# Input stage in another order, with the input's residual scaled in DRAM's copy later, in a hybrid decoder layer

## The chip, the cores and the metric

One core of one Trainium2 chip runs the whole layer. The metric is the time of one execution in microseconds (us) of device time, as the median of several runs. The kernel before takes 1295.74 us, median of 3 runs (1294.87 to 1296.15).

## What is computed

The input is x (1 x 1024 x 1024, fp32), ahead of which 16 meta tokens are put, so 1040 rows in all. One layer runs over them; its parts, cut to what matters here:

```python
h = layer_norm(concat([meta, x]), in_ln_g, in_ln_b)
z = h @ w_in + b_in
q, k, v, c_in, gates = split(z)                       # 512, 128, 128, 1024, 2048 columns
y_attn = sliding_window_attention(q, k, v) @ w_attn_proj
c = c_val * sigmoid(c_gate)                           # the halves of c_in
y_conv = silu(layer_norm(causal_dwconv(c, 31 taps))) @ w_conv_proj
mixed = sigmoid(g_attn) * y_attn + sigmoid(g_conv) * y_conv
h = layer_norm(ALPHA * h + mixed @ w_out)             # ALPHA = 2 ** 0.25
f = (gelu(g) * u) @ ffn_w_down                        # u, g: conv3 of h @ ffn_w_up
out = layer_norm(ALPHA * h + f)                       # meta rows dropped
```

The change touches the way from x to h and to the first tiles of z, and the way from h to the term ALPHA * h, called the residual here.

## The kernel before, in words

Activations stand transposed for the products (channels on the 128 partitions, tokens along the free axis). Nearly all products run in three passes of fp32r matmuls: each operand is split into a high part, rounded to fp32r, and a low part, the rest; high times high, low times high and high times low are summed in PSUM. A split is thus a CAST and a subtraction for each operand: for activations both on DVE, for weights the cast on ACT and the subtraction on POOL (`split`, L282 and L285; in the input stage `wsplit0`, L491 and L493). A plain fp32 matmul (`raw=True`, L512) needs no split and shows two records in the trace.

A scheduler deals each engine's instructions by priority: `tc.cur_priority`, set ahead of each section and in `rank(...)` blocks; a lower number goes first, and `after(a, b)` fixes an order by hand. In the input stage the order on DVE, ACT and TensorE is written out by hand (`in_order`, `dv`, `ac`, `pe`). All loads, and stores written as `load(dram, sbuf)`, are issued in order on SP's queue (L113); `store` issues on ACT's (L117). A transfer that waits holds all behind it on its queue.

**Input stage (L171 to L560).** The rows of x come as eight blocks of 128 tokens (`load_x`), the meta tokens as a ninth, `xm`. A block's statistics (`stat`, two BN_STATS and an aggregate on DVE; `half_stat` does one half of it), an ACT table lookup and Newton steps (`table`, `newton`) give mean and rate, `norm` writes the normalised rows `xn` on DVE or ACT. `turns` transposes them on TensorE (L463), `scaled` applies the norm's gain and bias on ACT while leaving PSUM (L469, into `tm`), `parts` splits them (L479 the cast, L484 the subtraction on DVE, L482 on POOL) into RHO and RHC, the halves of h transposed, by channel blocks k = 0 to 7. Tokens go in three groups, `HG`: 272, 384 and 384 columns. Meanwhile `z_first` makes the first three column tiles of z: tile 0 is k, tile 1 is v, tile 2 is the first quarter of q (L515, or L512 raw); `evac` takes a finished tile out of PSUM. In group 0 only k runs raw, while the splits are made; v and q follow, v's weights arriving first. In group 1 v and q run together, and k behind them; in group 2 one tile after the other. POOL makes four low parts of group 2 and all three weights' low parts.

**Residual, before.** gb holds the norm's gain and bias on all partitions (1 MB, loaded in the start). Behind the input stage `residual` scales gb by ALPHA once (L269), turns each block of x in place into ALPHA * h by two operations of 128x1024 on DVE (L271, L272), and stores it in DRAM's h0d. h0d is read back as `OB<-h0d` for the product with w_out. x's buffers belong to the start's pools, whose memory goes to the convolution's input `cin` and to attention's tiles when they close.

**Convolution, gates, attention (L640 to L985).** Their tiles of z (`z_tile`, L309, L312 and L313 for the three passes, with 400, 384 and 256 columns), the taps on DVE (L677), attention on all engines.

**Projections (L1040 to L1115).** For each of eight output blocks m the joined weights w_attn_proj and w_conv_proj (`w_ab[m]`, 512 KB) are loaded and split. For each of four token groups g (`PG`, 258 or 256 columns) `branch` makes two products: attention's (PSUM tag "mm", three buffers) and the convolution's (tag "t", two buffers). `merge` loads both gates of the block from DRAM (sgd, `OB<-sgd` or `FA<-sgd`, 256 KB), then on DVE: gate times product one (L1084), gate times product two (L1085), their sum (L1086), and the split of the result, ACT's half (L1093) and DVE's subtraction (L1094). At m < 4 w_out's blocks are loaded besides.

Of the kernel before, what the change touches and what calls it, by code (L numbers as in the profile page):

```python
# [29 lines left out]
P = 128  # L30
# [34 lines left out]
RK_TURN, RK_SPLIT, RK_EVAC, RK_START, RK_QKV, RK_RESID, RK_ATT = 450, 500, 600, 1000, 10000, 20000, 30000  # L65
RK_CLN, RK_OSPLIT, RK_Z, RK_CONV, RK_PROJ = 38000, 39000, 40000, 60000, 70000
# [35 lines left out]
def tile_hybrid_layer(  # L102
# [89 lines left out]
    for j in range(NB):  # L192
        with rank((10, 11, 15, 17, 18, 20, 21, 22)[j]):
            load_x(j)
# [28 lines left out]
    nc.vector.tensor_scalar(qb, colA[:, 0:4], HD ** -0.5, None, OP.mult)  # L223

    nc.vector.tensor_scalar(colA[:, 10:30], colA[:, 10:30], 0.5, None, OP.mult)
# [3 lines left out]
    nc.vector.tensor_scalar(nsink, sink, -1.0, None, OP.mult)  # L229
# [32 lines left out]
    gb = sp.tile([P, 2, D], F, name="gb")  # L262
    load(gb[:, :, :].rearrange("p a b -> p (a b)"), dram(ln0_in, 0, [[0, P], [1, 2 * D]]))
    gb_scaled = []

    def residual(src, mu, rs, n, first, dst):
        if not gb_scaled:
            gb_scaled.append(1)
            after(nc.vector.tensor_scalar(gb, gb, ALPHA, None, OP.mult), last_split[3])  # L269
        src = src[:n]  # L270
        nc.vector.scalar_tensor_tensor(src, src, mu[:n], gb[:n, 0], OP.subtract, OP.mult)  # L271
        nc.vector.scalar_tensor_tensor(src, src, rs[:n], gb[:n, 1], OP.mult, OP.add)  # L272
        load(dst, src[first:n])

# [15 lines left out]
    def weights(shape, fill):  # L290
# [4 lines left out]
        with rank({1: 14, 2: 13, 3: 16, 4: 23}.get(n, RK_SPLIT)):  # L295
            last_fill.append(fill(raw))
# [94 lines left out]
    norms, xns, later = {}, {}, []  # L391
# [42 lines left out]

    def norm(t, j, on_dve):
# [3 lines left out]
        xns[j] = sp.tile([P, D], F, name="xn", tag="xn", bufs=4) if j >= 0 else xm  # L439
        to = xns[j] if j >= 0 else xm[96:]  # L440
# [6 lines left out]
        later.append((x_, mv[:n, i, 0:1], r_[:n, i:i + 1], n, j))  # L447
# [72 lines left out]

    def evac(g, *tiles):
        for i in tiles:
            a, b = span(i, g)
            with rank(RK_EVAC):
                evacs0[i](g, a, b, sums0[i])
# [8 lines left out]
    table(1)  # L534
    newton(1)
# [3 lines left out]
    wsplit0(1, True)  # L539
# [7 lines left out]
    parts(0, 0, 1)  # L547
    stat(2, 4)
    scaled(0, 5)
    wsplit0(2, True)  # L550
    scaled(0, 6, 7)
    z_first(0, (0,), 5, 6, 7, raw=True)
    table(2)
    parts(0, 2, 3, 4)
# [3 lines left out]
    norm(2, 4, True)  # L558
    evac(0, 0)
    parts(0, 5, 6, 7)  # L560
    z_first(0, (1,), 0, 1)
    for k in range(2, 6):
        z_first(0, (1,), k)
        z_first(0, (2,), k - 2)
    turns(1, 0, 1, 2, 3)
    scaled(1, 0, 1, 2, 3)
    wsplit0(0, True)
    z_first(0, (1,), 6)
    z_first(0, (2,), 4)
    z_first(0, (1,), 7)  # L570
    evac(0, 1)
    z_first(0, (2,), 5)
    turns(1, 4, 5, 6, 7)
    z_first(0, (2,), 6, 7)
    evac(0, 2)
    parts(1, 0, 1)
    scaled(1, 4, 5, 6, 7)
    half_stat(3, 5, 0)
    parts(1, 2)
    half_stat(3, 5, 1)  # L580
    parts(1, 3)
    half_stat(3, 6, 0)
    parts(1, 4)
    half_stat(3, 6, 1)
    parts(1, 5)
    half_stat(3, 7, 0)
    parts(1, 6)
    half_stat(3, 7, 1)
    table(3)
    parts(1, 7)  # L590
# [4 lines left out]
    for k in range(8):  # L595
        z_first(1, (1, 2), k)
    evac(1, 1, 2)
    z_first(1, (0,), 0, 1)
    turns(2, 0, 1, 2, 3)
    scaled(2, 0, 1, 2, 3)  # L600
    parts(2, 0, 1, 2, 3, on_pool=(1, 3))
    z_first(1, (0,), 2, 3, 4, 5)
    turns(2, 4, 5, 6, 7)
    scaled(2, 4, 5, 6, 7)
    parts(2, 4, 5, 6, 7, on_pool=(5, 7))
    z_first(1, (0,), 6, 7)
    evac(1, 0)
# [503 lines left out]
    for k in range(4):  # L1111
        prep_wo(k, early[k])
# [638 lines left out]
```

## Time and profile before

| what | value |
|---|---|
| median of 3 runs | 1295.74 us (1294.87 to 1296.15) |
| the profiled execution, its own time | 1294.77 us |
| its span in the trace | 1293.0 us |
| TensorE busy | 1264.6 us |
| DVE busy | 1086.4 us |
| ACT busy | 578.5 us |
| POOL busy | 66.5 us |
| moved by DMA | 212.10 MB |

The profile is one execution on the chip. PE is TensorE, DVE is VectorE, POOL is GpSimd, SP issues transfers; "SPq" is its queue of instructions. A line of a timeline has start and duration in us, engine, line of the kernel, operation, what it writes and reads, shape, count, and in brackets the idle time of the engine ahead of it with what ended it. A line of waits has engine, line and tile that waited, what it waited for, and the total, the count and the longest in us. A line of windows has the stretch, its length, each engine's busy time with the number of instructions (PE, PEld, DVE, ACT, POOL), the granted clock of TensorE, DMA's share and GB/s. Lines of DMA issues have what is written and read, queue, count, KB each, and the median us from issue to landing. The chain of waits is followed back from the last instruction to what released it.

### The profile page before, as it was taken

The numbers are of one execution on the slowest core, as the hardware profiler recorded it, in microseconds if no ns is written. First come the engines' busy times: TensorE is split into PE (matmuls) and PEld (weight loads), VectorE is DVE, ScalarE is ACT, GpSimd is POOL, SyncE is SP. The second block draws the span as 40 slices with busy tenths as digits, with TensorE's granted clock in tenths as the row PEclk, the third lists the DMA queues.
The fourth block names the chain that finished last, engine by engine and source line by source line (L and its number), as shares of the span: only waits on it lengthen the run. The fifth ranks groups of instructions, "written<-read, shape, count | busy, mean of one in ns | idle before, by whom it ended". The sixth has DMA issues, their size and how long they took to land.

```text
span 1293.0 us, 21590 instructions
## 1 busy us (share of the span) xinstructions
PE 1264.6 (98%) x8506; PEld 1186.6 (92%) x8506; DVE 1086.4 (84%) x1834; ACT 578.5 (45%) x1049; POOL 66.5 (5%) x35
## 2 busy tenths in 40 slices
PE   5999999999999999999999999999999999999997
PEld 5889999999999999788899999999999997788886
DVE  7888999999979676637899989988889876987697
ACT  4422244545554222345565554554455543535330
POOL 2200000001112232000000000000000000000000
PEclk9999999999999999999999999999999999999999
DMA  6265743433255565222135555453454566989712
GB/s 247 82 237 139 184 119 88 109 88 99 68 135 162 157 168 134 75 79 98 66 131 181 198 192 191 176 205 121 158 209 158 192 228 243 392 288 359 259 67 81
DMA packets 96008, 212.10 MB, mean 164 GB/s; under 512 B 10771, under 2 KB 35923, under 8 KB 95650
## 3 DMA queue, kind: packets, MB, share of 16 engines
q1 hardware_dynamic: 84138, 199.64, 46.3%
q10 hardware_dynamic: 11768, 11.08, 2.6%
q8 instruction: 66, 1.08, 0.4%
q14 instruction: 36, 0.29, 0.1%
HBM read 150.29 MB, written 62.70 MB: 165 GB/s over the span
## 4 chain that ended last, share of the span: by engine, by line
PE 89%; DVE 5%; DMA 4%; ACT 1%; SPq 1%; issue 0%; POOL 0%; DVEq 0%; ACTq 0%
PE px L1472 14%; PE py L1472 9%; PE ps_x L1597 9%; PE ps_z L312 7%; PE ps_z L309 7%; PE ps_z L313 7%; PE ps_z L1597 6%; PE pz L1472 5%; PE pw L1472 5%; PE ps_p L312 2%; PE ps_p L313 2%; PE ps_p L309 2%; PE ps_w L309 2%; PE ps_w L313 2%; PE ps_w L312 2%; PE ps_t L859 1%
## 5 line engine op out<-in xcount | busy, mean ns | idle before, releaser
L677 DVE SCALAR_TENSOR_TENSOR FA<-cin,cols,FA 128x1026 f32<-128x1026 f32 x120 | 154.8, 1300 | 0.2
L309 PE MATMUL ps_z<-RHO,whi 128*128 128x384 f32 (+2 forms) x324 | 104.3, 322 | 2.3 <-DVE cin L668 2.3
L312 PE MATMUL ps_z<-RHO,whi 128*128 128x384 f32 (+2 forms) x324 | 104.9, 324 | 0.0
L312 PE MATMUL ps_z<-RHC,whi 128*128 128x384 f32 (+2 forms) x324 | 104.6, 323 | 0.0
L309 PE MATMUL ps_z<-RHC,whi 128*128 128x384 f32 (+2 forms) x324 | 104.6, 323 | 0.0
L313 PE MATMUL ps_z<-RHO,wlo 128*128 128x384 f32 (+2 forms) x324 | 104.2, 322 | 0.0
L313 PE MATMUL ps_z<-RHC,wlo 128*128 128x384 f32 (+2 forms) x324 | 103.7, 320 | 0.0
L1294 DVE TENSOR_TENSOR RHO<-wr,RHO 128x512 fp32r<-128x512 f32 x94 | 63.5, 684 | 10.9 <-ACT RHO L1293 10.9
L1293 ACT CAST RHO<-wr 128x512 fp32r<-128x512 f32 x94 | 56.6, 619 | 18.6 <-DVE wr L1311 10.1
L282 ACT CAST whi<-wr 128x1024 fp32r<-128x1024 f32 x37 | 38.8, 1050 | 55.9 <-PE ps_z L312 33.5
L309 PEld LDWEIGHTS ps_z<-RHO,whi 128*128 128x128 f32 x324 | 60.9, 188 | 2.9 <-DVE cin L668 2.6
L312 PEld LDWEIGHTS ps_z<-RHC,whi 128*128 128x128 f32 x324 | 60.9, 188 | 0.6
L309 PEld LDWEIGHTS ps_z<-RHC,whi 128*128 128x128 f32 x324 | 60.8, 188 | 0.5
L313 PEld LDWEIGHTS ps_z<-RHO,wlo 128*128 128x128 f32 x324 | 60.9, 188 | 0.3
L313 PEld LDWEIGHTS ps_z<-RHC,wlo 128*128 128x128 f32 x324 | 61.0, 188 | 0.2
L312 PEld LDWEIGHTS ps_z<-RHO,whi 128*128 128x128 f32 x324 | 60.9, 188 | 0.4
L1311 DVE TENSOR_TENSOR wr<-wr 128x512 f32<-128x512 f32 x88 | 60.1, 683 | 0.2
L285 POOL TENSOR_TENSOR wlo<-wr,whi 128x1024 fp32r<-128x1024 f32 x17 | 42.1, 2479 | 186.6 <-ACT whi L282 173.6
L684 ACT ACTIVATE FA<-ps_z,cols 128x386 f32<-128x386 f32 (+2 forms) x48 | 26.1, 544 | 52.7 <-PE ps_z L313 45.0
L1484 ACT COPY FA<-px 128x514 f32<-128x514 f32 (+2 forms) x23 | 13.2, 572 | 81.3 <-PE px L1472 81.3
L1294 DVE TENSOR_TENSOR ws<-wr,ws 128x512 fp32r<-128x512 f32 x60 | 40.6, 684 | 6.1 <-ACT ws L1293 6.0
L1472 PE MATMUL px<-OA,RHO 128*128 128x258 f32 x324 | 43.5, 283 | 0.0
(452 smaller groups left out, 3593.9 us busy)
## 6 DMA issues: line engine op xcount, KB each, us to landing
wr<-in_w_up_dram SPq DMA_DIRECT2D x44, 512.0 KB, 4.1
wr<-in_w_z_dram SPq DMA_DIRECT2D x30, 512.0 KB, 3.3
fd<-FA SPq DMA_DIRECT2D x44, 256.0 KB, 2.4
OB<-in_w_down_dram SPq DMA_DIRECT2D x21, 512.0 KB, 5.0
FA<-sd SPq DMA_DIRECT2D x15, 512.0 KB, 8.8
qt<-qd SPq DMA_DIRECT2D x28, 256.0 KB, 4.1
td<-OB SPq DMA_DIRECT2D x12, 512.0 KB, 3.4
sums<-fd SPq DMA_DIRECT2D x12, 512.0 KB
```

The source lines that it names most:

```text
L282: ins = nc.scalar.copy(hi, raw)
L285: return (nc.vector if quick else nc.gpsimd).tensor_tensor(lo, raw, f32(hi), OP.subtract)
L309: ins = nc.tensor.matmul(ps, ah, bh, start=i == 0, stop=False)
L312: nc.tensor.matmul(ps, ah, bl, start=False, stop=False)
L313: last = nc.tensor.matmul(ps, al, bh, start=False, stop=i == n - 1)
L677: nc.vector.scalar_tensor_tensor(acc[c], cin[:, j:j + U], wc, acc[c], OP.mult, OP.add)
L684: nc.scalar.activation(t, ps, AF.Tanh, bias=bcol(14 + i), scale=0.5)
L1293: nc.scalar.copy(hi, src)
L1294: ins = nc.vector.tensor_tensor(lo, src, f32(hi), OP.subtract)
L1311: ins = nc.vector.tensor_tensor(*x)
L1472: ins = nc.tensor.matmul(o, x[:, ks], bmat(sub, q, hl, k), start=first and k + j == 0, stop=k == 3 and j == 2, skip_group_check=not first)
L1597: nc.tensor.matmul(banks[i], l[:, ts], r[:, ws], start=first and a and x + k == 0, stop=z and x == len(ops) - 1 and k == 2, skip_group_che ...
```

## The change

- **Loads.** Before: x0, x1, columns, v's weights, k's, x2, q's, x3 to x7. After: x0, x1, columns, k's weights, x2, x3, q's, v's, x4 to x7. The load of gb in the start is gone.
- **Order of the input stage.** q's first token group runs raw, directly behind k's; v comes last in group 0. v's low weights are made on DVE, q's and k's on POOL. Statistics are taken by whole blocks. In groups 1 and 2 the three tiles run in one interleaved loop, `lagged`, each two channel blocks behind the one before. In group 2 POOL makes no low parts any more; ACT makes four casts in its place. Three small scalings of constants move behind the first table lookup.
- **Rows to DRAM.** `norm` stores the normalised rows, without gain and bias, to h0d at once. The last four blocks of normalised rows stand in OB, not in the four buffers of `xn`.
- **Residual.** `residual(i, behind)` runs inside `merge`, at the 16 places of RES_AT: (1,0), (1,2), (2,0), (2,2), and g = 0, 1, 2 of m = 3 to 6. Each takes one half (512 channels) of a block: a load from h0d (256 KB), a multiplication by gb and an addition on DVE, and a store back to its place. At the first of each half, gb's half of gain and bias is loaded (2 x 256 KB) and scaled, and the two meta rows are done as well. There are two buffers for the rows. The loads have the merges' rank.

The added operations' places in DVE's order, as the scheduler deals them: gb's scaling and the first half block (with the meta rows) stand ahead of the first merge of all, then come one in m = 1 (at g = 3), two in m = 2, three in m = 3 (g = 1, 2, 3), two in m = 4 with gb's second scaling, two in m = 5, three in m = 6, the last two in m = 7. The multiplication stands between L1086 and L1094 of a merge or next to them, the addition beside it. On SP's queue the half blocks' stores and loads stand between the gate loads, w_ab's and w_out's.

```diff
-RK_TURN, RK_SPLIT, RK_EVAC, RK_START, RK_QKV, RK_RESID, RK_ATT = 450, 500, 600, 1000, 10000, 20000, 30000
-RK_CLN, RK_OSPLIT, RK_Z, RK_CONV, RK_PROJ = 38000, 39000, 40000, 60000, 70000
+RK_TURN, RK_SPLIT, RK_EVAC, RK_START, RK_QKV, RK_VROW, RK_ATT = 450, 500, 600, 1000, 10000, 20000, 30000
+RK_CLN, RK_OSPLIT, RK_Z, RK_CONV, RK_PROJ, RK_RESID = 38000, 39000, 40000, 60000, 70000, 200000
...
     for j in range(NB):
-        with rank((10, 11, 15, 17, 18, 20, 21, 22)[j]):
+        with rank((10, 11, 14, 15, 18, 20, 21, 22)[j]):
             load_x(j)
...
-    gb = sp.tile([P, 2, D], F, name="gb")
-    load(gb[:, :, :].rearrange("p a b -> p (a b)"), dram(ln0_in, 0, [[0, P], [1, 2 * D]]))
-    gb_scaled = []
-
-    def residual(src, mu, rs, n, first, dst):
-        if not gb_scaled:
-            gb_scaled.append(1)
-            after(nc.vector.tensor_scalar(gb, gb, ALPHA, None, OP.mult), last_split[3])
-        src = src[:n]
-        nc.vector.scalar_tensor_tensor(src, src, mu[:n], gb[:n, 0], OP.subtract, OP.mult)
-        nc.vector.scalar_tensor_tensor(src, src, rs[:n], gb[:n, 1], OP.mult, OP.add)
-        load(dst, src[first:n])
...
-        with rank({1: 14, 2: 13, 3: 16, 4: 23}.get(n, RK_SPLIT)):
+        with rank({1: 13, 2: 17, 3: 16, 4: 23}.get(n, RK_SPLIT)):
...
+    def scalings():
+        dv(V.tensor_scalar(qb, colA[:, 0:4], HD ** -0.5, None, OP.mult))
+
+        dv(V.tensor_scalar(colA[:, 10:30], colA[:, 10:30], 0.5, None, OP.mult))
+        dv(V.tensor_scalar(nsink, sink, -1.0, None, OP.mult))
+
     def norm(t, j, on_dve):
         x_, n = src_of(j)
         i = tokens[t].index(j)
         mv, t_, r_, m_ = norms[t]
-        xns[j] = sp.tile([P, D], F, name="xn", tag="xn", bufs=4) if j >= 0 else xm
-        to = xns[j] if j >= 0 else xm[96:]
+        if j < 0:
+            xns[j], to = xm, xm[96:]
+        else:
+            xns[j] = to = sp.tile([P, D], F, name="xn", tag="xn", bufs=4) if j < 4 else OB[:, (j - 4) * D:(j - 3) * D]
         for a in range(0, D, 512):
             if on_dve:
                 dv(V.tensor_scalar(to[:, a:a + 512], x_[:, a:a + 512], r_[:n, i:i + 1], m_[:n, i:i + 1], OP.mult, OP.add))
             else:
                 ac(nc.scalar.activation(to[:, a:a + 512], x_[:, a:a + 512], AF.Identity, bias=m_[:n, i:i + 1],
                                         scale=r_[:n, i:i + 1]))
-        later.append((x_, mv[:n, i, 0:1], r_[:n, i:i + 1], n, j))
+        load(*((h0d[2 + j * P:2 + (j + 1) * P, :], to) if j >= 0 else (h0d[0:2, :], xm[96 + U0:96 + NMETA])))
...
+    def lagged(g, tiles, steps):
+
+        for t in steps:
+            for l, i in enumerate(tiles):
+                if 0 <= t - 2 * l < KC:
+                    z_first(g, (i,), t - 2 * l)
+                    if t - 2 * l == KC - 1:
+                        evac(g, i)
...
+    scalings()
     newton(1)
     norm(1, 0, True)
     norm(1, 1, False)
     turns(0, 0, 1, 2, 3)
-    wsplit0(1, True)
     stat(2, 2, 3)
     scaled(0, 0)
     z_first(0, (0,), 0, raw=True)
         scaled(0, k + 1)
         turns(0, k + 4)
         z_first(0, (0,), k + 1, raw=True)
-    parts(0, 0, 1)
+    scaled(0, 5, 6)
+    parts(0, 0)
     stat(2, 4)
-    scaled(0, 5)
-    wsplit0(2, True)
-    scaled(0, 6, 7)
+    table(2)
+    scaled(0, 7)
     z_first(0, (0,), 5, 6, 7, raw=True)
-    table(2)
-    parts(0, 2, 3, 4)
+    parts(0, 1)
     newton(2)
     norm(2, 2, True)
     norm(2, 3, False)
     norm(2, 4, True)
+    z_first(0, (2,), *range(8), raw=True)
     evac(0, 0)
-    parts(0, 5, 6, 7)
-    z_first(0, (1,), 0, 1)
-    for k in range(2, 6):
-        z_first(0, (1,), k)
-        z_first(0, (2,), k - 2)
+    wsplit0(1)
+    parts(0, 2, 3, 4, 5)
     turns(1, 0, 1, 2, 3)
     scaled(1, 0, 1, 2, 3)
+    z_first(0, (1,), 0, 1, 2, 3)
+    evac(0, 2)
+    parts(0, 6, 7)
+    turns(1, 4, 5, 6, 7)
+    z_first(0, (1,), 4, 5, 6, 7)
+    evac(0, 1)
+    parts(1, 0, 1)
+    wsplit0(2, True)
+    scaled(1, 4, 5, 6, 7)
+    stat(3, 5)
+    parts(1, 2, 3)
     wsplit0(0, True)
-    z_first(0, (1,), 6)
-    z_first(0, (2,), 4)
-    z_first(0, (1,), 7)
-    evac(0, 1)
-    z_first(0, (2,), 5)
-    turns(1, 4, 5, 6, 7)
-    z_first(0, (2,), 6, 7)
-    evac(0, 2)
-    parts(1, 0, 1)
-    scaled(1, 4, 5, 6, 7)
-    half_stat(3, 5, 0)
-    parts(1, 2)
-    half_stat(3, 5, 1)
-    parts(1, 3)
-    half_stat(3, 6, 0)
-    parts(1, 4)
-    half_stat(3, 6, 1)
-    parts(1, 5)
-    half_stat(3, 7, 0)
-    parts(1, 6)
-    half_stat(3, 7, 1)
+    stat(3, 6)
+    parts(1, 4, 5)
+    stat(3, 7)
+    parts(1, 6, 7)
     table(3)
-    parts(1, 7)
     newton(3)
     norm(3, 5, True)
     norm(3, 6, False)
     norm(3, 7, True)
-    for k in range(8):
-        z_first(1, (1, 2), k)
-    evac(1, 1, 2)
-    z_first(1, (0,), 0, 1)
+    lagged(1, (1, 2, 0), range(9))
     turns(2, 0, 1, 2, 3)
     scaled(2, 0, 1, 2, 3)
-    parts(2, 0, 1, 2, 3, on_pool=(1, 3))
-    z_first(1, (0,), 2, 3, 4, 5)
+    parts(2, 0, 1, 2, 3, hi_act=(1, 3))
+    lagged(1, (1, 2, 0), range(9, 11))
     turns(2, 4, 5, 6, 7)
+    lagged(1, (1, 2, 0), range(11, 12))
     scaled(2, 4, 5, 6, 7)
-    parts(2, 4, 5, 6, 7, on_pool=(5, 7))
-    z_first(1, (0,), 6, 7)
-    evac(1, 0)
-    for i in range(3):
-        z_first(2, (i,), *range(8))
-        evac(2, i)
+    parts(2, 4, 5, 6, 7, hi_act=(5, 7))
+    lagged(2, (0, 1, 2), range(12))
     first_nm = dv_done[-1]
 
-    tc.cur_priority = RK_RESID + 1000
+    tc.cur_priority = RK_VROW
     vrow = sp.tile([NH, J_LEN], F, name="vrow")
...
-    tc.cur_priority = RK_RESID
-    for src, mu, rs, n, j in later:
-        if j >= 0:
-            residual(src, mu, rs, n, 0, h0d[2 + j * P:2 + (j + 1) * P, :])
-        else:
-            residual(src, mu, rs, NMETA, U0, h0d[0:2, :])
     start.close()
...
+    res_stack = ExitStack()
+    res_p = res_stack.enter_context(tc.tile_pool(name="res", bufs=1, side="left", reuse_waits="tile"))
+    RES_AT = [(m, g) for m in range(1, 7) for g in ((0, 2) if m < 3 else (0, 1, 2))]
+    res_gb = []
+
+    def residual(i, behind):
+        h, j = divmod(i, NB)
+        hs = slice(h * 512, (h + 1) * 512)
+        pieces = [((3, 7, 2, 6, 0, 4, 1, 5)[j], P)] + ([(-1, 2)] if j == 0 else [])
+        if j == 0:
+            res_gb[:] = [res_p.tile([P, 2, 512], F, name="gb", tag="gb")]
+            with rank(RK_EVAC):
+                for q in range(2):
+                    load(res_gb[0][:, q], dram(ln0_in, q * D + h * 512, [[0, P], [1, 512]]))
+            behind = nc.vector.tensor_scalar(res_gb[0], res_gb[0], ALPHA, None, OP.mult)
+        gb = res_gb[0]
+        for tile_, n in pieces:
+            rows = h0d[2 + tile_ * P:2 + (tile_ + 1) * P, hs] if tile_ >= 0 else h0d[0:2, hs]
+            t = res_p.tile([P, 512], F, name="res", tag="res", bufs=2)[:n]
+            with rank(RK_EVAC):
+                load(t, rows)
+            for op, q in ((OP.mult, 0), (OP.add, 1)):
+                ins = nc.vector.tensor_tensor(t, t, gb[:n, q], op)
+                after(ins, behind)
+                behind = ins
+            load(rows, t)
...
-                nc.vector.scalar_tensor_tensor(mixed2(g, m, 1), v, 0.5, f32(h), OP.mult, OP.subtract)
+                last_dve = nc.vector.scalar_tensor_tensor(mixed2(g, m, 1), v, 0.5, f32(h), OP.mult, OP.subtract)
+            if (m, g) in RES_AT:
+                residual(RES_AT.index((m, g)), last_dve)
             return ins, last_act
...
+    res_stack.close()
```

More of the change, by code (lines that the diff above doesn't have):

```diff
@@ L222, in tile_hybrid_layer @@
     qb = const.tile([P, 4], F, name="qb")
-    nc.vector.tensor_scalar(qb, colA[:, 0:4], HD ** -0.5, None, OP.mult)
-    nc.vector.tensor_scalar(colA[:, 10:30], colA[:, 10:30], 0.5, None, OP.mult)
     half_ = const.tile([P, 1], F, name="half")
@@ L228, in tile_hybrid_layer @@
     nsink = const.tile([P, NH], F, name="nsink")
-    nc.vector.tensor_scalar(nsink, sink, -1.0, None, OP.mult)
     def ln_stats(srcs, pool=None, tag="", bufs=4, behind=None, half_stats=None):
@@ L390, in tile_hybrid_layer @@
     tokens = [(-1,), (0, 1), (2, 3, 4), (5, 6, 7)]
-    norms, xns, later = {}, {}, []
+    norms, xns = {}, {}
     def src_of(j):
```

## The prediction

> **What bounds the kernel now.** First the page: busy shares, then the shares of the chain that ended last.
>
> ```profile
> PE 1264.6 (98%) x8506; PEld 1186.6 (92%) x8506; DVE 1086.4 (84%) x1834; ACT 578.5 (45%) x1049; POOL 66.5 (5%) x35
> ...
> PE 89%; DVE 5%; DMA 4%; ACT 1%; SPq 1%; issue 0%; POOL 0%; DVEq 0%; ACTq 0%
> ```
>
> TensorE is busy for all but 28 us of 1293.0, and the chain runs through it. The change takes next to nothing from TensorE's work, so it can win only where TensorE waits, and can lose wherever it makes TensorE wait. Next, therefore, TensorE's waits (times in us: total, count, longest):
>
> ```profile
> PE ps_h L463 <- DMA cols<-in_cols_dram: 8.3, 1, 8.3
> PE ps_h L463 <- DVE xn L443: 2.9, 1, 2.9
> PE ps_z L309 <- DVE cin L668: 2.3, 1, 2.3
> PE ps_z L515 <- DVE RHC L479: 1.8, 1, 1.8
> PE pw L1472 <- ACT FA L1274: 0.9, 1, 0.9
> PE ps_t L859 <- ACT pmT L782: 0.7, 1, 0.7
> ```
>
> The first two are the first loads and norms, whose order stays. The third is the bubble ahead of the first convolution tile, the fourth lies in the input stage; these two the change touches. Between 100 us and the projections nothing over 0.7 us can be won.
>
> **Part 1, the input stage: from 12 to 65 us.** A busy TensorE isn't a dense one here; what sets the pace is DVE, which splits each transposed column block (a CAST and a TENSOR_TENSOR), takes the statistics and norms. Rows of the timeline of DVE (start, duration):
>
> ```profile
> 14.45 1.29 DVE L405 BATCH_NORM_STATS2 st<-x 128x6 f32<-128x512 f32 x2 [0.95 <-DMA x<-in_x_dram]
> 15.77 0.21 DVE L406 BATCH_NORM_AGGREGATE mv<-st 128x2 f32<-128x12 f32 x1
> 15.89 0.27 DVE L479 CAST RHO<-FA 128x272 fp32r<-128x272 f32 x1
> ...
> 16.55 0.29 DVE L479 CAST RHO<-FA 128x272 fp32r<-128x272 f32 x1
> ...
> 22.71 0.15 DVE L430 SCALAR_TENSOR_TENSOR t<-mv,r 128x3 f32<-128x3 f32 x1
> ...
> 23.49 1.91 DVE L443 TENSOR_SCALAR xn<-x,r,m 128x512 f32<-128x512 f32 x4
> ...
> 30.23 0.36 DVE L479 CAST RHO<-tm 128x384 fp32r<-128x384 f32 x1 [2.77 <-ACT tm L469]
> ...
> 31.10 0.35 DVE L479 CAST RHO<-tm 128x384 fp32r<-128x384 f32 x1
> ...
> 32.94 2.77 DVE L484 TENSOR_TENSOR RHO<-tm,RHO 128x384 fp32r<-128x384 f32 x1
> ...
> 57.73 1.23 DVE L285 TENSOR_TENSOR wlo<-wr,whi 128x1024 fp32r<-128x1024 f32 x1 [2.75 <-ACT whi L282]
> ```
>
> Prices: statistics of one block 1.5 us (1.29 and 0.21); a split of 272 columns 0.66 (15.89 to 16.55), of 384 columns 0.87 (30.23 to 31.10); newton 0.8 (22.71 to 23.49); two blocks normed 1.9; a split that meets a weight split on POOL 2.77 where about 0.6 is usual (0.87 less the cast's 0.35, rounded up), 2.2 more; a weight's low half on DVE 1.2 (57.73). The stage ends on TensorE:
>
> ```profile
> 33.37 0.51 PE L515 MATMUL ps_z<-RHO,whi 128*128 128x384 f32 x2
> ...
> 33.90 0.51 PE L515 MATMUL ps_z<-RHO,whi 128*128 128x384 f32 x2
> ...
> 45.91 1.47 PE L463 MATMUL ps_h<-cols,xn 128*128 128x128 f32 x12
> ...
> 64.98 0.34 PE L309 MATMUL ps_z<-RHO,whi 128*128 128x400 f32 x1
> ```
>
> One k-step (three matmuls) takes 0.53 us (33.37 to 33.90), twelve transposes 1.47, and the first matmul after the stage starts at 64.98.
>
> Now the same walk in the new order. With x3 loaded ahead of q's weights the 0.95 wait falls away: the statistics are done at 15.0. Then split 0 (15.7), block 4 (17.2), split 1 (17.8), newton (18.6), norms (20.5), v's low half on DVE (1.2) and about 0.8 of waiting for ACT's high half (an allowance of mine) to 22.5, six splits at 0.66 and one small subtraction of 0.5 (27.0), split (1,0) (27.9), split (1,1) with a POOL lock (31.0), block 5 (32.5), two splits (34.3), block 6 (35.8), split (1,4) with k's POOL lock (38.9). TensorE has then done 6 of the 48 k-steps of groups 1 and 2, since tiles start two steps apart; the other 42 are 22.3 us, 24 transposes 2.9, end 64.1; with half a lock fewer (a lock's length depends on where the split meets it) 63.0. I take 63.0: **gain 2.0**. The later splits (0.87, against 1.6 us of matmuls for one step of three tiles) don't bind. Ends: a whole lock missed and the other halved, 4.2; both whole and a slow clock, 0 (after the next rows).
>
> ```profile
> 18.21 2.00 PE L512 MATMUL ps_z<-FA,wr 128*128 128x272 f32 x8
> ...
> 25.66 1.07 PE L515 MATMUL ps_z<-RHC,whi 128*128 128x272 f32 x2 [1.84 <-DVE RHC L479]
> ...
> 27.41 2.41 PE L463 MATMUL ps_h<-cols,xn 128*128 128x128 f32 x12
> ```
>
> q's first group in fp32 is eight k-steps of two records each: eight records took 2.00, so it is at most 4.0 us of TensorE in place of 24 split matmuls, in a stretch where DVE is late: nothing. As to the clock: after 1.84 us of idleness the twelve transposes took 2.41 against 1.47: a stretch at a lower clock. In the new order TensorE is short of work around 29 to 32.5 us; a slow stretch behind that ends while DVE is still late, unless it reaches past 38.9; I leave it out of the sum. For the low end both locks are whole (64.1) and twelve transposes lose their 0.94 once: 0.
>
> [...]
>
> **Part 2, the residual's old place.** Rows of DVE's timeline, then of the chain and of TensorE's timeline:
>
> ```profile
> 61.33 9.64 DVE L271 SCALAR_TENSOR_TENSOR x<-x,mv,gb 128x1024 f32<-128x1024 f32 x8
> ...
> 77.29 6.05 DVE L272 SCALAR_TENSOR_TENSOR x<-x,r,gb 128x1024 f32<-128x1024 f32 x5
> ```
> ```profile
> 83.59 6.48 DMA h0d<-x
> ...
> 91.23 0.45 PE L309 MATMUL ps_z<-RHO,whi 128*128 128x400 f32 x1 [2.29 <-DVE cin L668]
> ```
>
> Sixteen operations of 1.2 us and a few smaller ones, some 20 us of DVE, end at 83.3, the last store starts at 83.59 and lands 6.48 later; cin, whose memory is that of the start's buffers, is written only then, and TensorE waits 2.29. In the new order the rows are stored from the norms, before 45 us, and no residual runs here: **gain 2.3**, at most that, and at least 1.3 should vrow's turn or ACT's evacuation be the next to be late by up to 1.
>
> **Part 3, the residual's new place.** 16 half blocks, each a load of 256 KB, two TENSOR_TENSORs (128x512) and a store, all on SP's queue, between the merges of m = 1 to 7; the two of gain and bias are loaded and scaled twice. One projection m, seen in POOL's, DVE's timeline, the line of an equal TENSOR_TENSOR, and the DMA issues (KB each, us to landing):
>
> ```profile
> 443.73 2.40 POOL L285 TENSOR_TENSOR wlo<-wr,whi 128x1024 fp32r<-128x1024 f32 x1 [9.09 <-ACT whi L282]
> 455.21 2.40 POOL L285 TENSOR_TENSOR wlo<-wr,whi 128x1024 fp32r<-128x1024 f32 x1 [9.09 <-ACT whi L282]
> ```
> ```profile
> 444.45 1.96 DVE L1094 SCALAR_TENSOR_TENSOR RHC<-FA,RHC 128x256 fp32r<-128x256 f32 x1
> ...
> 447.89 0.42 DVE L1094 SCALAR_TENSOR_TENSOR RHO<-OB,RHO 128x256 fp32r<-128x256 f32 x1
> ...
> 449.85 0.42 DVE L1084 SCALAR_TENSOR_TENSOR OB<-OB,ps_p 128x256 f32<-128x256 f32 x1 [0.55 <-PE ps_p L313]
> ```
> ```profile
> 443.73:455.21 11.48, 11.48 (x98) 11.48 (x98) 7.95 (x17) 2.75 (x7) 2.39 (x1) 1.00 0.38 95
> ```
> ```profile
> L1641 DVE TENSOR_TENSOR r<-r,b x16: 678/682/693, 1110.1 to 1175.3; 128x512 f32<-128x512 f32 x16
> ```
> ```profile
> wr<-in_w_ab_dram SPq DMA_DIRECT2D x7, 512.0 KB, 5.9
> ...
> OB<-sgd SPq DMA_DIRECT2D x21, 256.0 KB, 3.2
> ...
> fd<-FA SPq DMA_DIRECT2D x44, 256.0 KB, 2.4
> ```
>
> A projection lasts 11.48 us (443.73 to 455.21), in which DVE is busy 7.95. Half a block adds 2 x 0.68 = 1.36. In DVE's order two halves stand in most m: 7.95 + 2.7 = 10.7, which fits; in m = 3 and 6 three: 12.0, 0.6 too much. The 16 halves come to 21.8 us, gain and bias to about 2, and all but some 1.2 of it lies in DVE's idle 3.5 per m. A merge may run late by about 3.8: its second product's PSUM is used again two column groups on, 2 x 2.87 (a quarter of 11.48 each) less that product's own 1.44, less the 0.5 that it takes anyway. So load alone stalls nothing.
>
> Waits can. Each half waits for its load; with two buffers the load waits until the store of the half before last has landed. The multiply and add stand in DVE's queue ahead of a merge's last operation and of the next merge; whoever waits behind them is TensorE, for PSUM. Also POOL's split holds operations that read two buffers (1.96 against 0.42). A cycle of a buffer is load 3.2, operations 1.4, store 2.4, issues 0.4 = 7.4 us for two halves that are 5.74 (two column groups) to 11.48 apart. Where two halves follow within 5.74, a wait of up to 1.7; where such an operation then meets POOL's lock it runs 2.4 late besides and 1.36 itself: 5.4 in all against 3.8, a stall of 1.6. DVE's order has that at m = 3 and 6 and where gain and bias are loaded anew (m = 4), and not all meet the lock: ends 0 and 4.8. I take one of three, **loss 1.5**.
>
> [...]
>
> **Part 4, the rest.** Attention and convolution come out in another order; TensorE waits under 1 us there and DVE has those 20 us less ahead of it: 0, ends -0.7 (the ps_t wait gone) and +1.5 (a new wait of the bubble's kind).
>
> **Sum.** -2.0 - 2.3 + 1.5 = -2.8 against the profiled run's 1294.77 (span 1293.0 and 1.77 around it): 1292.0. That run lies 0.97 under the median of the three, 1295.74; against the median I forecast **1293.0**. Its own range, with the ends above: 1290.5 to 1296. The measurement of this kernel can tell about 0.2%, 2.6 us, from no change.
>
> **The rivals.** *A, the projections hide it all and a lock misses.* Loads land in 2.4, like the stores, and one POOL split passes between DVE's: -4.3 to -6.5, 1289.2 to 1291.4, say 1290.5. For it: 3.5 us idle per m; against: gate loads at 3.2 in the same queue.
>
> *B, the new queue starves the merges (slower).* The loads stand on SP's queue among the projections' 512 KB weights, which land after 5.9. At such a landing a cycle is 5.9 + 1.4 + 2.4 + 0.4 = 10.1 for two halves, 81 us for 16, while the stretch from m = 1 to halfway through m = 7 is 6.5 x 11.48 = 75. DVE stands 6 us, nearly all of it passed to TensorE, beside the 1.5: -4.3 + 7.5 = +3.2, 1299.0. It decides from a landing of 75/8 - 4.2 = 5.2 us on. For it: the weights' row; against: gate loads of equal size, same queue, same stretch, take 3.2.
>
> *C, the input stage gains nothing.* Both locks whole and the slow clock: 0 - 2.3, and 3 lost in the projections: +0.7, 1296.4. For it: the lock at 32.94 was whole before too; against: DVE waits for a load no more.
>
> **How the numbers follow.** Forecast 0.42, A 0.25, B 0.21, C 0.12. Of the forecast's own range a little over half lies more than 2.6 under 1295.74 (0.23 of 0.42), the rest within; C is within but for 0.02. Faster 0.25 + 0.23 = 0.48; slower 0.21 + 0.02 = 0.23; within 0.2% the other 0.29. The range takes most of A and B's middle: 1288.5 to 1299.5.
>
> **What would show it.** Part 1: the first 400-column matmul starts at 62 to 64 instead of 64.98. Part 2: TensorE's wait for cin is gone and DVE has no 1.2 us operations between 59 and 83. Part 3: in the projections TensorE waits for DVE (an operation of a merge) 1 to 3 times, under 2 us each; half-block loads land in 3 to 4 us; m stays at 11.5 elsewhere. Wrong, if the stage ends at 65 or later, if half-block loads take over 5.2, or if TensorE waits over 2 us in attention or convolution.

## The result and the profile after

The changed kernel takes 1309.99 us, median of 4 runs (1308.64 to 1310.95), beside 1295.3 for the kernel before: ratio 1.0112, 95% interval 1.0095 to 1.013. It is slower by 14.7 us, outside the range that was given (1288.5 to 1299.5). Its profiled execution took 1308.64, with a span of 1306.8.

Busy times on the page, then TensorE's waits (us in total, times, longest):

```profile
PE 1269.9 (97%) x8498; PEld 1189.9 (91%) x8498; DVE 1085.3 (83%) x1854; ACT 582.5 (45%) x1055; POOL 59.7 (5%) x30
```
```profile
PE ps_p L292 <- DVE OB L1092: 8.1, 6, 3.0
PE ps_w L295 <- DVE OA L268: 3.5, 1, 3.5
...
PE ps_p L292 <- DVE OB L1091: 0.8, 1, 0.8
```

The wait for cin is gone; 12.4 us of waits for DVE are new, all in the projections and at the start of the product with w_out (L1091, L1092 are a merge's two products, L268 the split of w_out). TensorE is also busy 5.3 us longer, all of it between the two landmarks below and with the same 1236 matmuls (192.2 us busy before, 197.5 after). Where the time went shows in two landmarks, the first matmuls of the projections and the last ones of the product with w_out (the two times are the first and the last start); before, then after:

```profile
L309 PE MATMUL ps_p<-OA,whi x128: 279/281/283, 431.0 to 516.8; 128*128 128x256 f32 x96, 128*128 128x258 f32 x32
...
L309 PE MATMUL ps_w<-OA,RHO x32: 392/394/483, 579.9 to 623.2; 128*128 128x512 f32 x32
```
```profile
L292 PE MATMUL ps_p<-OA,whi x128: 279/282/418, 427.3 to 524.3; 128*128 128x256 f32 x96, 128*128 128x258 f32 x32
...
L292 PE MATMUL ps_w<-OA,RHO x32: 393/396/477, 593.7 to 637.1; 128*128 128x512 f32 x32
```

The projections start 3.7 us earlier, and the product with w_out ends 13.9 later: 3.7 gained ahead, 17.6 lost between. Behind it nothing changes (the last difference is 1306.8 - 1293.0 = 13.8). The longest projection matmul took 418 ns where 283 was the longest before: part of the loss is clock. Rows of TensorE's timeline around its three longest waits, then windows of the changed kernel (busy times of PE, PEld, DVE, ACT, POOL, then the granted clock):

```profile
477.29 0.28 PE L295 MATMUL ps_p<-OA,whi 128*128 128x256 f32 x1
477.41 0.28 PE L296 MATMUL ps_p<-OA,wlo 128*128 128x256 f32 x1
479.56 0.38 PE L292 MATMUL ps_p<-OC,whi 128*128 128x256 f32 x1 [1.87 <-DVE OB L1092]
479.78 0.28 PE L295 MATMUL ps_p<-OC,whi 128*128 128x256 f32 x1
...
509.83 0.38 PE L292 MATMUL ps_p<-OC,whi 128*128 128x256 f32 x1 [2.98 <-DVE OB L1092]
...
534.75 0.50 PE L295 MATMUL ps_w<-OA,RHC 128*128 128x512 f32 x1 [3.45 <-DVE OA L268]
```
```profile
481.00:484.00 3.00, 3.00 (x17) 3.00 (x16) 2.97 (x5) 1.35 (x3) 2.08 (x1) 0.51 0.75 202
...
510.00:513.00 3.00, 3.00 (x26) 3.00 (x27) 1.33 (x4) 0.42 (x1) 0.00 (x0) 1.00 0.96 215
...
536.00:539.00 3.00, 3.00 (x10) 2.42 (x9) 3.00 (x5) 0.00 (x0) 0.00 (x0) 0.50 0.03 7
```

Behind two of the waits (1.87 us before 479.56, 3.45 before 534.75) the clock fell to one half (0.50), 1.4 and 0.9 us after TensorE had started again, and stayed there for some 3.4 us: about 481.0 to 484.4 and 535.6 to 539.0, read off in windows of 1 us. Behind a third (2.98 before 509.83) it stayed at 1.00. By an estimate from the clock each low stretch loses half its length, 1.7 us, 3.4 together; by the matmuls' starts, 0.21 us apart there for 128x256 and 0.12 at 1.00, it is 1.5. So of the 17.6, 12.4 are waits and, by the clock, 3.4 its low stretches. Most of the other 1.8 goes by what breaking the stream costs, by an estimate from the rows above: in the stream a matmul starts 0.12 after the one before it (477.29, 477.41), but the last one ahead of a wait runs its whole 0.28, and the one behind it is followed only after 0.22 (479.56, 479.78), so 0.16 + 0.10 = 0.26 for each of the eight waits, some 2 us.

What DVE waited for, what SP's queue waited for from 395 to 545 us, and SP's own instructions around 475 us:

```profile
DVE res L1019 <- DMA res<-h0d: 15.0, 9, 2.9
...
DVE gb L1011 <- DMA gb<-in_ln_dram: 6.5, 2, 3.3
```
```profile
SPq L113 <- DMA h0d<-res: 31.7, 13, 4.0
```
```profile
471.11 0.32 SPq L113 DMA_DIRECT2D h0d<-res  x1
472.36 0.37 SPq L113 DMA_DIRECT2D OB<-sgd  x1
475.20 0.32 SPq L113 DMA_DIRECT2D res<-h0d  x1
475.61 0.38 SPq L113 DMA_DIRECT2D h0d<-res  x1
476.09 0.38 SPq L113 DMA_DIRECT2D OB<-sgd  x1
```

A store issued at 471.11 holds its buffer until it has landed, 4.08 us later; the load into that buffer stands at the head of SP's queue until 475.20, and the next store and the next gate load (`OB<-sgd`) are issued only behind it. The chain of waits and DVE's timeline continue from there:

```profile
471.11 4.08 DMA h0d<-res
475.20 3.19 DMA res<-h0d
478.48 0.69 DVE res L1019
```
```profile
478.48 0.69 DVE L1019 TENSOR_TENSOR res<-res,gb 128x512 f32<-128x512 f32 x1 [2.92 <-DMA res<-h0d]
479.09 0.41 DVE L1092 SCALAR_TENSOR_TENSOR OB<-OB,ps_p 128x256 f32<-128x256 f32 x1
```

DVE stands 2.92 us at the multiplication; the merge's L1092, for which TensorE needs no residual, is behind it in the queue. TensorE's wait of 1.87 ended there. Thirteen such waits of SP came to 31.7 us.

### The profile page after: what moved, and what is told of

Read it like the earlier page. It is cut to its first block, busy times and chain, and to the rows that moved or that the text cites. A ratio compares the mean times of both kernels' runs of the same rounds, so it can differ in the third digit from the quotient of the medians.

```text
span 1306.8 us, 21668 instructions
## 1 busy us (share of the span) xinstructions
PE 1269.9 (97%) x8498; PEld 1189.9 (91%) x8498; DVE 1085.3 (83%) x1854; ACT 582.5 (45%) x1055; POOL 59.7 (5%) x30
## 4 chain that ended last, share of the span: by engine, by line
PE 87%; DVE 6%; DMA 5%; ACT 1%; issue 1%; SPq 0%; DVEq 0%; ACTq 0%
PE px L1482 14%; PE py L1482 9%; PE ps_x L1607 9%; PE ps_z L295 8%; PE ps_z L292 8%; PE ps_z L296 8%; PE ps_z L1607 6%; PE pz L1482 5%; PE pw L1482 5%; PE ps_w L295 2%; PE ps_w L296 2%; PE ps_w L292 2%; DMA res<-h0d 2%; PE ps_z L506 1%; DMA h0d<-res 1%; PE ps_t L837 1%
## 5 line engine op out<-in xcount | busy, mean ns | idle before, releaser
L1304 DVE TENSOR_TENSOR RHO<-wr,RHO 128x512 fp32r<-128x512 f32 x94 | 63.7, 686 | 10.4 <-ACT RHO L1303 10.2
L265 ACT CAST whi<-wr 128x1024 fp32r<-128x1024 f32 x37 | 38.8, 1049 | 52.8 <-PE ps_z L295 37.3
L268 POOL TENSOR_TENSOR wlo<-wr,whi 128x1024 fp32r<-128x1024 f32 x17 | 42.9, 2524 | 212.5 <-ACT whi L265 212.5
L1494 ACT COPY FA<-px 128x514 f32<-128x514 f32 (+2 forms) x23 | 13.2, 573 | 80.2 <-PE px L1482 80.2
L292 PE MATMUL ps_p<-OC,whi 128*128 128x256 f32 (+1 forms) x128 | 37.0, 289 | 8.1 <-DVE OB L1092 8.1
```

The source lines that it names most:

```text
L265: ins = nc.scalar.copy(hi, raw)
L268: return (nc.vector if quick else nc.gpsimd).tensor_tensor(lo, raw, f32(hi), OP.subtract)
L292: ins = nc.tensor.matmul(ps, ah, bh, start=i == 0, stop=False)
L1304: ins = nc.vector.tensor_tensor(lo, src, f32(hi), OP.subtract)
```

## The experiments

Times are medians; each is compared with the kernel before as it ran beside it on the same chip, so differences are given to that; where two runs are subtracted from each other, it is their medians.

**The late residual left out.** Edit: the call in `merge`.

```diff
-            if (m, g) in RES_AT:
-                residual(RES_AT.index((m, g)), last_dve)
```

> The changed kernel without the late residual: no half blocks are loaded, scaled or stored, so h0d keeps the plain normalised rows (gain, bias and ALPHA are left out of the residual). The changed kernel's trace starts its projections 3.7 us earlier than before and ends them 13.9 later, a loss of 17.6 between. Both theories: the loss is gone, 1295.3 - 3.7 = 1291.6. If part of the loss isn't the residual's (the new order of the rest, w_out's splits), 1294 to 1300.

1290.96 against 1295.25, ratio 0.9967 (0.9954 to 0.998): 4.3 faster than before, 19.0 faster than the change. The whole loss is the late residual's; the rest of the change gains.

**Its operations alone.** Edit: two blocks loaded once, no other transfer.

```diff
-            t = res_p.tile([P, 512], F, name="res", tag="res", bufs=2)[:n]
-            with rank(RK_EVAC):
-                load(t, rows)
...
+            t = res_t[i % 2][:n]
...
-            load(rows, t)
```

> The late residual's DVE operations alone: all 32 multiplications and additions and both scalings of gain and bias stay, but on two blocks that are loaded once, with no store and no further load (h0d keeps unscaled rows; that part of the computation is left out). Theory Q, SP's queue: the loss comes from transfers that wait at the queue's head for one another, so 1292 to 1294.5. Theory D, DVE's order and POOL's lock: operations in the merges' way cost it, so 1303 to 1309.

1296.72, ratio 1.0009 (0.9999 to 1.0019): 5.8 above the kernel without a late residual, between the two expectations. TensorE waited once at length. DVE and TensorE there:

```profile
488.90 1.78 DVE L1011 TENSOR_SCALAR gb<-gb 128x1024 f32<-128x1024 f32 x1 [2.62 <-DMA gb<-in_ln_dram]
```
```profile
492.94 0.38 PE L292 MATMUL ps_p<-OC,whi 128*128 128x256 f32 x1 [3.21 <-DVE OB L1093]
```
```profile
494.00:498.00 4.00, 4.00 (x23) 4.00 (x22) 4.00 (x12) 0.93 (x3) 0.00 (x0) 0.58 0.62 215
```

DVE stands at the scaling of the second halves' gain and bias, which can be loaded only once the first halves have done with the buffer; TensorE waits 3.21 us and then runs at 0.58 of the clock over 4 us, 1.7 us lost by the estimate from the clock.

**Its transfers alone.** Edit: the loop over multiplication and addition taken out.

```diff
-            for op, q in ((OP.mult, 0), (OP.add, 1)):
-                ins = nc.vector.tensor_tensor(t, t, gb[:n, q], op)
...
```

> The late residual's transfers alone: all half blocks are loaded and stored again, with two buffers, without the 32 multiplications and additions (gain, bias and ALPHA are left out of the residual). Theory Q: each load still stands at the head of SP's queue until the store before last has landed, now without DVE's time between, and gate loads behind it are late: 1298 to 1308. Theory D: 1291 to 1293.

1296.36, ratio 1.0009 (1.0 to 1.0019): 5.4 above the kernel without. That is under what the queue theory gave and above what the other did. DVE's waits from 440 to 500 us:

```profile
DVE OB L1087 <- DMA OB<-sgd: 10.9, 4, 3.7
```

In the kernel before, DVE's waits in the projections hold none for a gate load; here four merges wait, since those loads stand behind the half blocks'. Two stalls of TensorE (2.12 and 1.79) follow, and one low stretch of the clock, behind the second. So operations cost 5.8, transfers 5.4, and both together 19.0: neither theory alone, 7.8 more come from their coupling.

**Four buffers.** Edit: two more buffers in a free stretch of FA.

```diff
-            t = res_p.tile([P, 512], F, name="res", tag="res", bufs=2)[:n]
...
+            t = (res_p.tile([P, 512], F, name="res", tag="res", bufs=2)[:n] if o < 2 else
+                 FA[:n, 5120 + (o - 2) * 512:][:, :512])
```

> The changed kernel with four buffers for half blocks instead of two (two more in a free stretch of FA; two loads of w_out are moved by a few columns for it). A load then waits for the store of four halves before, which has landed long since. Theory Q: most of the 17.6 comes back, 1292.5 to 1297, and SP's waits for h0d stores fall from 31.7 to under 5. Theory D: unchanged, 1307 to 1311.

1296.84, ratio 1.0013 (1.0003 to 1.0022): 13.2 of the 19.0 are back, with all operations, all transfers and the same places. The 13.2 are the coupling's 7.8 and the transfers' own 5.4: what is left is what the operations cost alone. The coupling is the two buffers. SP's waits for the stores were expected under 5:

```profile
SPq L113 <- DMA h0d<-res: 14.8, 7, 4.2
...
SPq L113 <- DMA h0d<-FA: 8.2, 4, 2.8
```

The second line is that of the two buffers in FA, so these waits fell only from 31.7 to 23.0, and the expected number was wrong; what counts is that DVE hardly waits for half blocks any more (1.2 and 0.4 us in place of 15.0). What is left is again the stall at the second gain and bias (3.19 of TensorE).

**Gain and bias loaded once**, with four buffers:

```diff
-        if j == 0:
+        if i == 0:
```

> Four buffers as in the run with +5.8, and gain and bias loaded and scaled once, so that the second halves take the first halves' gain and bias (their own are left out). If the rest of the loss is the load for which DVE stands 3.4 us with the merges behind it: 1291 to 1292.5. If it is DVE's load: 1295.5 to 1297.

1294.26 against 1294.38, ratio 0.9998 (0.9989 to 1.0007). About 3 of the 5.8 (by the medians 2.6) are this load's; the other 3 remain, between the two expectations again. Windows of this kernel and of the hybrid below, same stretch:

```profile
450.00:500.00 50.00, 48.31 (x401) 47.91 (x400) 47.42 (x89) 12.32 (x26) 16.91 (x6) 1.00 0.80 233
```
```profile
450.00:500.00 50.00, 50.00 (x420) 50.00 (x419) 42.39 (x81) 13.85 (x29) 17.07 (x7) 1.00 0.67 191
```

DVE is busy 47.42 of 50 us: three halves per m fill it. TensorE waits three times, under 1 us each, and its clock stays at 1.00. Whether DVE's load alone makes these waits isn't shown: SP's queue still stands for stores here, too.

The traces measure the same without the other stages: the time between the two landmarks (192.2 us in the kernel before and without a late residual), beside TensorE's waits for DVE there and the low clock:

| kernel | above 192.2 | waits | low clock |
|---|---|---|---|
| the change | 17.6 | 12.4 in 8 | 3.4 |
| operations alone | 6.0 | 3.9 in 2 | 1.7 |
| transfers alone | 6.2 | 3.9 in 2 | 1.7 |
| four buffers | 6.0 | 3.9 in 2 | 1.7 |
| four buffers, gain and bias once | 3.3 | 2.5 in 3 | 0 |

The low clock stands there by that estimate too. With the 0.26 for each wait the two columns account for every loss within 0.3. By this measure the coupling is 5.4, not 7.8.

**Even places.** Edit: two halves ahead of the merges, then two per m, two buffers, gain and bias for both halves early.

```diff
-    RES_AT = [(m, g) for m in range(1, 7) for g in ((0, 2) if m < 3 else (0, 1, 2))]
+    RES_AT = [None] * 2 + [(m, g) for m in range(7) for g in (0, 2)]
...
```

> The whole computation, two buffers as in the change, but two halves ahead of the merges and then two in each m of 0 to 6 (g = 0 and 2), and gain and bias of both halves loaded and scaled ahead of the merges. So far: without the late residual 1291.0, its operations alone +5.7, its transfers alone +5.4, both with four buffers +5.8, with two +19.0. Theory P, places: two of three parts are the chain store, landing, load, landing through two buffers at three halves per m, and the anew loaded gain and bias, so 1291 to 1293.5. Theory S, the sheer load of DVE and of SP's queue, wherever it is put: 1296 to 1299.

1303.75, ratio 1.0069 (1.0052 to 1.0086): a miss for the places theory. DVE waited 2.97 us at the late load of the second gain and bias ahead of the merges, the halves bunched behind it, and with two buffers DVE waited for half blocks five times (9.0 us). Between the two landmarks it lost 12.6. It doesn't tell the sheer load from a bad start.

**All of it in the product with w_out**, behind the load of the rows that is made there anyway:

```diff
...
             load(whole, h0d[u:u + n, :])
+            gained(whole, n)
...
```

> The whole computation; the late residual leaves the projections and goes to the product with w_out, where the rows of h0d are read back anyway: two operations of 128x1024 on each block behind that load, no transfer besides the 1 MB of gain and bias. DVE was busy 25 of 50 us there. Theory P: 1291 to 1293.5 if the stage takes 21 us more of DVE's work without TensorE waiting. Theory S, DVE's load counts wherever it is put: 1296 to 1300, with TensorE waiting for DVE in the product with w_out or behind it.

1300.41, ratio 1.0041 (1.0026 to 1.0056). The projections lost nothing (the product with w_out starts at 516.6, without a late residual at 517.2), but at the stage's end TensorE stood:

```profile
PE ps_h L1253 <- DVE OB L1243: 5.7, 2, 4.8
```

L1243 is the last block's norm. The second theory's sign holds at that place, but DVE's load isn't all of it; the chain ahead of that norm is a round trip again:

```profile
605.14 4.61 DMA h1d<-OB
...
609.80 3.27 DMA OB<-h0d
```

The last block's rows are loaded into a buffer whose store has to land first; DVE stands 2.73 us for them, and only then come the two new operations. Behind the wait of 4.8 the clock was low once (0.59 from 622 to 626), about 1.7 us more by the same estimate.

**Half there, half here.** Six halves, one per m of 1 to 6, in DRAM's copy (blocks 4, 1, 5, which the product with w_out reads last); the other blocks behind its load.

```diff
...
+            if g == 0 and 1 <= m <= 6:
+                residual(m - 1, last_dve)
...
+            if i not in (4, 1, 5):
+                gained(whole, n)
```

> The whole computation. Six halves (the blocks that the product with w_out reads last) are scaled in DRAM's copy, one in each m of 1 to 6, through two buffers; the other five blocks and the meta rows are scaled behind the load that the product with w_out makes anyway; gain and bias are loaded and scaled once. Placing all in the product with w_out cost TensorE two waits at its end (5.7 in all, 1300.4), none in the projections. Theory P: neither place is overfull now, so 1290.5 to 1293. Theory S (DVE's and the queue's load counts wherever it is put): 1296 or more.

1292.0 against 1294.38, ratio 0.998 (0.9971 to 0.9989): the whole computation, faster than before by 2.4 and than the change by 17. TensorE waits for DVE in neither stage, and DVE is busy 42.39 of 50 in the projections.

**The input stage.** Four kernels without a late residual, the last of them the kernel before with only ps_v moved. First the new order with the residual in its old place:

```diff
+        later.append((x_, mv[:n, i, 0:1], r_[:n, i:i + 1], n, j))
...
+    for src, mu, rs, n, j in later:
...
```

> The changed kernel's input stage with the residual in its old place, behind that stage, on blocks of x, and nothing of it in the projections. If the gain of 4.3 that the kernel without a late residual shows (1291.0) is half the input order's and half the bubble's: 1293 to 1294.5, with the wait for cin at about 2.3. If the order of the input stage gives all of it: 1291. If nothing: 1295.3.

1306.24, ratio 1.0086 (1.0071 to 1.0101), which nothing had expected. Its waits and its chain:

```profile
PE ps_vm L714 <- DVE vmT L711: 7.0, 1, 7.0
PE ps_z L306 <- DVE cin L666: 2.8, 1, 2.8
```
```profile
79.65 10.54 DMA vd<-v1d
90.25 10.21 DMA h0d<-x
```

The bias row (v1d, expanded into vd) is now early, its transfer of 2.3 MB and the residual's stores run one behind the other, and what attention's start needs on DVE (kx) comes behind them: DVE waits 8.61 for the stores there. cin doesn't: it was written from 90.53 on, while the last store landed at 100.46.

The old order, without any residual:

```diff
-    lagged(1, (1, 2, 0), range(9))
+    for k in range(8):
+        z_first(1, (1, 2), k)
...
```

> The input stage in the order of before (loads, tiles, splits), rows stored to h0d at once, and no residual at all, neither early nor late (gain, bias and ALPHA are left out of it): beside 1291.0 it shows what the order of the input stage is worth by itself. By the stage's end (64.98 before, 63.85 after the change) 1292.1; by the prediction's 2.0, 1293; if the order is worth nothing, 1291.

1297.89, ratio 1.0022 (1.0013 to 1.0032). The bubble is there, though no residual is:

```profile
87.44 0.80 DVE L619 COPY vrow<-ps_v 8x400 f32<-8x400 f32 x2 [9.95 <-PE ps_v L618]
88.17 1.20 DVE L268 TENSOR_TENSOR wlo<-wr,whi 128x1024 fp32r<-128x1024 f32 x1
89.30 1.53 DVE L663 SCALAR_TENSOR_TENSOR cin<-ps_z,cols,FA 128x400 f32<-128x400 f32 x3
```
```profile
89.97 0.45 PE L292 MATMUL ps_z<-RHO,whi 128*128 128x400 f32 x1 [2.29 <-DVE cin L663]
```

DVE stands 9.95 us at the copy of the bias row, whose two matmuls TensorE makes only behind its first tile of 400 columns; a weight split and cin are queued behind it. Why this kernel's median lies 3.6 above before's, with less to do, was found only in part. Its profiled execution (1295.79) is one of its fastest: it has no low stretch of the clock, where the one of the kernel before stands at 0.50 for 3.4 us of the input stage (25.9 to 29.3), 1.7 us by the same estimate. It has the first load 0.8 us later and a second wait for cin of 0.9. The slower executions have no trace.

The same with those two matmuls directly behind the input stage:

```diff
-    tc.cur_priority = RK_VROW
+    tc.cur_priority = RK_QKV + 500
```

> The input stage in the order of before without any residual (gain, bias and ALPHA are left out), as in the run with 1297.9, and the bias row's two matmuls (ps_v) directly behind the input stage instead of behind the first tile of 400 columns. There, DVE stood 9.95 us at the copy of ps_v with the splits and cin behind it. If that place is what the order of the input stage is worth: 1291 to 1292.5, with no wait for cin. If the order of the stage's work itself counts: 1295.5 to 1298.

1291.2 against 1294.38, ratio 0.9973 (0.9964 to 0.9982), no wait for cin. In the changed kernel ps_v stands in that place, too; with the same rank, the old order let the scheduler put it behind the first tile. The matmuls' place is worth 6.7 by the medians, and 4.1 between the two traces, 0.8 of it the first load. It acts through DVE's order: with them early, cin stands ahead of the second weight split (82.61 and 90.90), above behind it. The order of the stage's other work is worth some 1.1 (3.2 under before here, 4.3 in the first experiment), which the intervals of the two don't tell from nothing.

The kernel before with ps_v alone moved:

```diff
-    tc.cur_priority = RK_RESID + 1000
+    tc.cur_priority = RK_QKV + 500
```

> The kernel before with only ps_v's two matmuls moved to directly behind the input stage; the whole computation, the residual in its old place. If the bubble of 2.29 hung on ps_v's place alone: 1292 to 1293.5. If the stores of the residual hold cin too, as the prediction had it: 1295 to 1297 (the two matmuls' place changes nothing, or the copy waits behind the residual on DVE).

1302.25, ratio 1.0057 (1.0043 to 1.0071), worse than either expectation:

```profile
PE ps_vm L716 <- DVE vmT L713: 4.3, 1, 4.3
...
PE ps_z L309 <- DVE cin L668: 2.8, 1, 2.8
```
```profile
89.57 1.22 DVE L285 TENSOR_TENSOR wlo<-wr,whi 128x1024 fp32r<-128x1024 f32 x1 [4.95 <-ACT whi L282]
...
98.23 1.57 DVE L697 CAST kx<-FA 128x1024 fp32r<-128x1024 f32 x4 [5.98 <-DMA h0d<-x]
```

The residual's stores again hold attention's start, kx. They don't hold cin: it stands in DVE's order right behind a weight split whose cast ACT makes only at 88.49, and is written at 90.71, with stores still landing. The early bias row pays only where the residual is gone, and the residual's removal pays only with the early bias row.

## Why the prediction was wrong

- **What bounds the kernel** held: it lost where TensorE came to wait, and by the low clock behind such waits, nowhere else.
- **Part 1, gain 2.0: the allowance of half a lock was wrong, the rest of the walk right.** DVE had split (1,4) done at 38.5 where the walk had 38.9, and TensorE came to the bias row at 63.85, where 64.98 was the end before: a gain of 1.1, inside the ends, and near the 64.1 that the walk gives without the allowance. Both of POOL's locks were whole: beside its weight splits (28.50 to 30.90, 35.35 to 37.71) a subtraction took 2.69 where 0.56 is usual, and a cast 2.13 where it otherwise takes 0.35:

```profile
28.62 2.69 DVE L475 TENSOR_TENSOR RHO<-tm,RHO 128x384 fp32r<-128x384 f32 x1
...
35.79 2.13 DVE L470 CAST RHC<-tm 128x384 fp32r<-128x384 f32 x1
```
```profile
63.85 1.12 PE L601 MATMUL ps_v<-tab 128*8 128x400 f32 x4
64.89 0.45 PE L292 MATMUL ps_z<-RHO,whi 128*128 128x400 f32 x1
```

  Over all runs the stage ended at 63.0 to 64.3 in the ten kernels with the new order, and at 63.7 to 65.0 in the four with the old.
- **Part 2, gain 2.3: right size, half the cause.** The last store's landing (90.07) was one of two things that ended late. The other is in DVE's timeline of the kernel before, and was not weighed:

```profile
88.70 0.80 DVE L618 COPY vrow<-ps_v 8x400 f32<-8x400 f32 x2 [4.22 <-PE ps_v L617]
89.43 1.20 DVE L285 TENSOR_TENSOR wlo<-wr,whi 128x1024 fp32r<-128x1024 f32 x1
```

  The bias row's copy and a weight split stand ahead of cin, until 90.6 as well. Removing either alone leaves a wait of 2.3 to 2.8. In the two runs that kept the stores cin was written while they were still landing, so there DVE's order alone held it. The change's list has ps_v's rank among its lines, and the prediction spoke of it only as a turn that might be late.
- **Parts 1 and 2 together** were 4.3 in the sum; the kernel without a late residual shows 4.3, and the trace of the change 3.7 at the start of the projections. That they agree is luck in part: part 1 came to 1.1, and attention's wait for pmT (0.7) is gone, which part 4 had only as an end. The forecast's own range wasn't the sum of its ends either, which give 1288.5 to 1300.7.
- **Part 3, loss 1.5, ends 0 and 4.8: the step that failed.** It measured 17.6 in the trace. Most of its prices were right: loads landed in 3.2, an operation took 0.69, and beside POOL's split up to 2.77; only stores took 2.9 (median) and not 2.4, in the chain above 4.08. What failed is "a cycle of a buffer is 7.4 us for two halves", and what was made of it. At three halves per m that is 11.1 of 11.48 us, with nothing spare, and 11.9 with the store's 2.9, which doesn't fit; the prediction took it for a wait of up to 1.7 in three places, each by itself. It left out that the load stands at the head of SP's queue for the landing of a store (31.7 us in 13 waits), that gate loads and the next stores stand behind it, so that each delay makes the next, and that TensorE's clock fell after some of its waits (3.4 of 17.6, by the estimate). Four buffers gave back 13.2 of 19.0. The second load of gain and bias was named, at up to 1.7; DVE waited 6.5 in two loads, over 3 at the second, which cost some 3 us with four buffers.
- **DVE's load** was taken as harmless by an average over m: 12.0 in two m, otherwise 10.7. With the coupling and the second load gone some 3 us were left, with DVE busy 47.42 of 50; that its load is their cause is argued, not shown.
- **Rival B** had the sign and the place, SP's queue, and a chance of 0.21. It set its point of decision by the landing time, 5.2, averaged over 75 us, and at 3.2 it ought not to have happened; by the trace the limit was local, around the m with three halves (the run with two per m, bunched behind a late load, lost too). Its price, 1299.0, was 11 short.
- **The clock** was weighed in the input stage, where a stretch of 3.4 us at 0.50 came before the change (25.9 to 29.3) and after it (33.9 to 37.3) alike, and not in the projections, where it did cost. With four buffers and gain and bias loaded once it stayed at 1.00 after three waits under 1 us. In the change it fell to 0.50 after a wait of 1.87 and stayed at 1.00 after one of 2.98; with only the transfers it stayed after 2.12 and fell after 1.79. So the length of a wait alone didn't decide it here; what did is open.

## What to carry to other kernels

A round trip through DRAM with two buffers isn't two transfers: count for the tightest place, not on average, the store's issue, its landing, the load's issue and landing, and whatever shares the issuing queue, since a transfer that waits at its head delays all behind it (13 such waits for a store came to 31.7 us here). Here it paid, 1292.0 us against 1309.99, to put work that is off the critical path where its data are loaded anyway and where DVE has slack (busy 42.39 of 50 us in the projections even so), a little in each stage. When a wait has a named releaser, look for a second one that ends almost as late: taking one away shows nothing until both are gone (here 2.3 to 2.8 us of the wait for cin were left with either one, none with neither).

## What was not expected of the hardware

A wait of TensorE cost more than itself: 12.4 us of waits brought two stretches of some 3.4 us at half the clock (0.50; a matmul took up to 418 ns against 283 for the same shape), 1.7 us more each by the clock, and by the estimate above 0.26 for each wait. Whether a wait of 1.8 to 3 us brought a low stretch differed from wait to wait: 1.79 and 1.87 did, 2.12 and 2.98 did not. Costs didn't add: operations 5.8 and transfers 5.4 apart, 19.0 together.
